# The opening of a transformer block on Trainium2: the modulation's last two column quarters multiplied in a row, the lower bounds in a buffer of their own, a sum in place of a maximum

## The chip, the cores and the metric

The kernel runs on one core of one Trainium2 chip. The metric is the device time of one execution in microseconds (us), the median of several executions. Five engines work side by side, each in the order of its own queue: TensorE (PE, matrix products and transposes, with its weight loads as PEld), VectorE (DVE), ScalarE (ACT), GpSimd (POOL) and SyncE (SP, which here only issues DMA transfers). They wait for each other through semaphores.

## The reference

One block of a diffusion transformer: 2048 tokens of width 1024, 256 tokens of context. A modulation vector is computed from a condition `c` (and from `c_ctx` for the context). It shifts and scales the normalized rows, which then go through a wide projection into two kinds of gated recurrences, an output projection, and a convolutional feed-forward part. What the change touches is the head of it:

```python
mod_x = (jax.nn.silu(c) @ w_mod[layer] + b_mod[layer])[:, None, :]
mod_c = jax.nn.silu(c_ctx) @ w_mod[layer] + b_mod[layer]
sh1, sc1, g1, sh2, sc2, g2 = jnp.split(mod_x, 6, axis=-1)
csh1, csc1, ... = jnp.split(mod_c, 6, axis=-1)
hx = _rmsnorm(x, norm1_g[layer]) * (1.0 + sc1) + sh1
feats_x = _mixer_features(hx, w_in[layer], lb, (rows, cols))   # p = h @ w_in, split into heads
```

`lb`, the lower bounds of the forget gates, is a softmax over two entries of `hgrn_lb`. The projection and the feed-forward products are done by the kernel with fewer block products (blocks of the operands are added and subtracted first), and each float32 operand is split into two float16 parts, so that a product is three float16 products.

## The kernel before

The rows are worked in four groups of 512 (`G`). The last group, rows 1536 to 2047 (called x3 here), is the first one used. Before the first projection can begin, the following is done.

- **Loads** (`setup`, `mod_loads`): SP issues, in this order, the first head's weights "z" (two tiles of `w_in`), the columns of `w_mod` that the first modulation needs in four quarters of 512 columns (`j4` = 2, 3, 0, 1; four tiles of 512 KB each), with x3 behind quarter 2 and the head's weights "q" and "vg" (three tiles, 1.5 MB) behind quarter 3. The context rows and the next group of rows come after.
- **Products** (`mod_first`, L284): eight per quarter, of the condition vectors against a weight tile, packed four at a time into 32-column strips of PE, in float32 (each shows as two instructions). The operand `silb` lies in a buffer with the tag "Tb".
- **Row copy and turn** (`mod_rows`, L249): ACT copies the quarter's result out of PSUM (L255, tile `modrow`), PE turns it into columns and adds the four strips (L260, `modt_ps`), DVE adds the bias and writes `modT` (L263). Quarters 0 and 1 give the shift, 2 and 3 the scale.
- **Lower bounds** (`lower_bounds`, L229): three DVE operations, an exponential on ACT, one small activation that brings the sigmoid's table back, and four DVE operations. Their buffer `tmp` has the tag "Tb" too, of which there is one.
- **Normalized rows** (`norm_rows`, L386): ACT squares x3 with sums (L398, eight), DVE adds them (L402), POOL takes the reciprocal root, DVE and ACT scale the rows (L409, L407).
- **Weights of the head** (`head_weights`, L720): per set, squares with sums on ACT (L749), a sum over the partitions on PE (`allsum`, L124), a power of two as scale (`pow2`, L112 to L116, on DVE), and then each block split into two float16 parts by ACT (L702, L759) and DVE (L703, L760), with sums and differences of blocks (L547 to L556) between.
- **Modulation** (`modulation`, L347): from `modT`, the factor U, a bound on the largest feature (`modq`, L361 to L369), its maximum over the partitions (`allmax`: a product with the identity, L138, a reduction, L140, and a product that spreads it, L142), and a power of two from it, `p2s`.
- **First features** (`first_blocks`, L419): eight groups of four transposes on PE (L416, three PSUM banks with the tag "pj"), each evicted with factor and shift by ACT (L459, six of them) or DVE (L457, two), in the order of blocks 0, 4, 1, 5, 2, 6, 3, 7; then the split of each block by ACT (L435, needs `p2s`) and DVE (L436), with block differences (L442). The first projection's products (L101 to L103) take these features.

The program is written in one order, and a planner then lays out each engine's queue from it: it plays the program against its own costs and gives an engine, at each moment, the earliest instruction of the program that is ready by that reckoning. On the chip each engine keeps the order so planned. `issue_after(i)` queues an instruction behind `i` on its engine, without a wait for its result. Tiles with the same tag share a fixed number of buffers, and a new tile waits until an older one has been read for the last time.

`heads` (L1038) calls these parts in the order: z weights; quarter 2 with its small vectors; lower bounds; x3's normalization; quarter 3; q and vg weights; quarter 0; quarter 1; modulation; first features.

Of the kernel before, what the change touches and what calls it, by code (L numbers as in the profile page):

```python
# [9 lines left out]
F32 = mybir.dt.float32  # L10
# [8 lines left out]
P = 128  # L19
# [4 lines left out]
NG = SEQ // G  # L24
# [26 lines left out]
def view(t, off, dims):  # L51
    return bass.AP(t.tensor, t.offset + off, [t.ap[0]] + dims)


class Kern:
# [173 lines left out]
    def lower_bounds(self):  # L229

        nc = self.nc
        a = view(self.sv, V_LB, [[8, 2], [1, 4]])
        b = view(self.sv, V_LB + 4, [[8, 2], [1, 4]])
        tmp = self.mp.tile([P, 24], F32, tag="Tb", bufs=1, name="tmp")
        m = tmp[:, 0:8].rearrange("p (d h) -> p d h", d=2)
        e = tmp[:, 8:24].rearrange("p (s d h) -> p s d h", s=2, d=2)
        nc.vector.tensor_tensor(m, a, b, ALU.max)
        nc.vector.tensor_tensor(e[:, 0], a, m, ALU.subtract)
        nc.vector.tensor_tensor(e[:, 1], b, m, ALU.subtract)
        nc.scalar.activation(e, e, AF.Exp)  # L240

        nc.scalar.activation(self.wp.tile([P, 1], F32, tag="rk", bufs=2, name="table"), e[:, 0, 0, 0:1], AF.Sigmoid)
        nc.vector.tensor_tensor(m, e[:, 0], e[:, 1], ALU.add)
        nc.vector.reciprocal(m, m)
        nc.vector.tensor_tensor(self.lb, e[:, 0], m, ALU.mult)
        nc.vector.tensor_scalar(self.omlb, self.lb, -1.0, 1.0, ALU.mult, ALU.add)


    def mod_rows(self, rows, nr, j4):  # L249


        nc = self.nc
        if nr == 2:
            rs = self.mp.tile([P, 512], F32, tag="Kl", bufs=KL, name="modrow")
            nc.scalar.copy(rs, rows)  # L255
            rows = rs
        ps = self.ps("tu", [P, 4, 2], "modt_ps")
        for j in range(4):
            sel = self.sel if nr == 2 else self.ones
            nc.tensor.matmul(ps[:, j, :nr], rows[:, j * P:(j + 1) * P], sel, start=True, stop=True, skip_group_check=True)  # L260
        o = self.modT[:, :nr, 4 * j4:4 * j4 + 4].rearrange("p d j -> p j d")
        bm = view(self.sv, V_BM + 4 * j4, [[1, 4], [0, nr]])
        nc.vector.tensor_tensor(o, ps[:, :, :nr], bm, ALU.add)  # L263

    def mod_loads(self):

        nc = self.nc
        self.items0[0][0]()
        self.wm = {}
        for j4, places in ((2, ("hx",) * 4), (3, ("hx",) * 4), (0, KEPT[:4]), (1, ("FG", "KTt", "ou0", "ou1"))):  # L270
            self.wm[j4] = []
            for k, tag in zip(range(0, KT, 2), places):
                w = self.slot_tile([P, 2, 512], F32, tag, "wm")
                nc.sync.dma_start(w, self.I["w_mod"][j4, :, k:k + 2])
                self.wm[j4] += [w[:, i] for i in range(2)]
            if j4 == 2:
                place = [h.rearrange("p k a t -> p (k a t)").bitcast(F32) for h in self.hc]
                place.append(self.slot_tile([P, G], F32, "qs", "x3"))
                self.x3 = self.load_rows(NG - 1, place)
            if j4 == 3:  # L280
                self.items0[4][0]()
                self.items0[5][0]()

    def mod_first(self, j4):  # L284

        nc = self.nc
        ps = self.ps("sc", [P, 512], "mod_ps")
        for k, w in enumerate(self.wm[j4]):
            q = k % 4 * B
            nc.tensor.matmul(ps[q:q + B], self.silb[:, k], w, start=k < 4, stop=k >= 4, skip_group_check=True)  # L290
        if j4 == 2:
            self.small_vectors()
        self.mod_rows(ps, 2, j4)

    def mod_later(self, j4):

# [50 lines left out]
    def modulation(self, cpool, pool, gain, sc, sh, dqcol, room=1.0):  # L347

        nc = self.nc
        n = gain.shape[-1]  # L350
        shp = list(sc.shape)
        A = cpool.tile(shp, F32, name=f"A{dqcol}")
        B = cpool.tile(shp, F32, name=f"B{dqcol}")
        U = pool.tile(shp, F32, tag="ra", bufs=4, name="modu")
        nc.vector.tensor_scalar(U, sc, 1.0, None, ALU.add)
        nc.vector.tensor_tensor(U, U, gain, ALU.mult)
        j = pool.tile(shp, F32, tag="ra", bufs=4, name="modj")
        q = pool.tile([P, 2], F32, tag="wdq", bufs=4, name="modq")
        ax = mybir.AxisListType.XY if len(shp) == 3 else mybir.AxisListType.X
        for i, (v, n) in enumerate(((U, 2.0 * D), (sh, 2.0))):  # L360
            nc.vector.scalar_tensor_tensor(j, v, n * room ** 2, v, ALU.mult, ALU.mult)  # L361
            nc.vector.tensor_reduce(q[:, i:i + 1], j, ax, ALU.add)
        if dqcol:

            sb = pool.tile([P, 1], F32, tag="edge", bufs=2, name="sumb")
            nc.vector.tensor_copy(sb, self.allsum(q[:, 1:2]))
            nc.vector.tensor_tensor(self.xx, self.allmax(q[:, 0:1]), sb, ALU.add)
            nc.vector.tensor_scalar(self.xx, self.xx, 1.03 / room ** 2, None, ALU.mult)
        nc.vector.tensor_tensor(q[:, 0:1], q[:, 0:1], q[:, 1:2], ALU.add)  # L369
        s, i = self.pow2(self.wp, self.allmax(q[:, 0:1]), 1, "w")  # L370
        nc.vector.tensor_copy(self.dqx[:, dqcol:dqcol + 1], i)
        self.plain = U, sh, s
        nc.vector.tensor_scalar(A, U, s, None, ALU.mult)
        nc.vector.tensor_scalar(B, sh, s, None, ALU.mult)
        return A, B, None
# [43 lines left out]
    def first_blocks(self, g, xn, places, bank, plain=False):  # L419
# [3 lines left out]
        nc = self.nc  # L423
# [20 lines left out]
        A, B, s = self.plain if plain else self.mod1  # L444
        late, b = [], []
        for k0 in (0, 2):
            f = [places[k0 + r]() for r in range(2)]
            units = [(slice(k0, k0 + 2), f)] if len(f[0]) == len(f[1]) == 1 else [(slice(k0 + i, k0 + i + 1), []) for i in range(2)]
            for i in range(2):
                k = k0 + i  # L450
                at = [(v[0][:, i] if len(v) == 1 else v[i])[:, :2 * n] for v in f]
                for r in range(2):
                    kk = k + 4 * r
                    tp = self.transposed(xn, kk, bank)
                    ka, kb = (v[:, which, kk:kk + 1] for v in (A, B))
                    if r and (g is None or plain and i):
                        nc.vector.tensor_scalar(at[r], tp, ka, kb, ALU.mult, ALU.add)  # L457
                    else:
                        nc.scalar.activation(at[r], tp, AF.Identity, bias=kb, scale=ka)  # L459
                if len(units) == 2 or i:  # L460
                    u = units[i if len(units) == 2 else 0][0]
                    both = [v[0][:, :, :2 * n] for v in f] if len(units) == 1 else [view(v, 0, [[0, 1], [1, 2 * n]]) for v in at]
                    b.append((u, [both[r][:, :, c * n:(c + 1) * n] for r in range(2) for c in range(2)]))
                    for r in range(2):
                        late.append((r, u, both[r][:, :, :n]))
                        if not plain:
                            pair(*late.pop())
                yield
# [569 lines left out]
    def heads(self):  # L1038

        nc, pool = self.nc, self.mp  # L1040
        W, items = self.W0, self.items0
        for _, comp in items[:4]:
            comp()
        self.mod_first(2)
        self.lower_bounds()
        self.norm_rows(NG - 1, self.x3)
        self.mod_first(3)
        for _, comp in items[4:]:
            comp()
        self.mod_first(0)  # L1050
        self.mod_first(1)
        place = [self.gate_tile() for _ in range(4)]
        xc = self.load_rows(None, place)
        self.mod1 = self.modulation(self.ep, pool, view(self.sv, V_N1, [[0, 2], [1, 8]]), self.modT[:, :, 8:16],
# [10 lines left out]
        rows = lambda g, tags: self.norm_rows(g, self.load_rows(g, [p() for p in self.places(tags, f"x{g}")]), self.tail)  # L1065
# [4 lines left out]
        for s in range(4 * 2 * NH):  # L1070
            h, i = divmod(s, NG)
# [922 lines left out]
```

## Time and profile before

| | |
|---|---|
| median of 3 executions | 2602.67 us (2600.81 to 2603.92) |
| profiled execution, its own time | 2600.32 us |
| its span, first to last instruction | 2598.5 us |
| mean granted TensorE clock | 0.985 |
| PE busy | 2509.5 us, 97% of the span |
| DVE busy | 1894.8 us, 73% |
| ACT busy | 1351.5 us, 52% |
| first product of the first projection | 55.04 us after the start |

How to read the lines: a timeline row gives the start and the duration in us, the engine, the line of the kernel, the operation, the tile written and the tiles read, the shapes, how many such instructions follow each other, and in brackets how long the engine had been idle and what ended that. A grouped row gives, after the bar, the busy time in us, the mean of one in ns, and the idle time ahead of it.

### The profile page before, as it was taken

The page shows a single profiled execution, that of the slowest core. Times are in us where ns is not written, and L with a number is a line of the kernel's source. Part 1 is how long each engine was busy: PE and PEld are TensorE (multiplying, and loading weights), DVE is VectorE, ACT ScalarE, POOL GpSimd, SP SyncE. Part 2 cuts the span into 40 slices and gives each one's busy share as a digit, 9 for nine tenths or more (in the row PEclk, how much of TensorE's full clock was granted, in tenths as well). Part 3 has the DMA queues.
Part 4 walks back from the last instruction along what each step waited for, and adds up shares of the span by engine and source line. Part 5 has one row for each costly group of instructions (what it writes and reads, how often), then busy time and mean ns, then how long its engine had stood idle before and what let it go on. Part 6 is the DMA issues. An engine that isn't in the chain of part 4 may idle for free.

```text
span 2598.5 us, 56251 instructions
## 1 busy us (share of the span) xinstructions
PE 2509.5 (97%) x22763; PEld 1655.1 (64%) x22763; DVE 1894.8 (73%) x4304; ACT 1351.5 (52%) x2880; POOL 383.0 (15%) x377
## 2 busy tenths in 40 slices
PE   6899998999999999999999999999999999999998
PEld 3688987889899999895544444444444444444443
DVE  5798686786878778885659787888888887223756
ACT  6886566564655454553647455556655554211221
POOL 1100000000000000001132343434443442000000
PEclk6999999999999999999999999999999999999999
DMA  7334342442558667794421333333333326544552
GB/s 304 118 114 153 119 144 87 136 155 67 180 163 280 213 220 251 247 331 148 169 82 43 128 104 108 101 111 114 102 106 110 122 90 246 196 173 154 211 212 84
DMA packets 144788, 402.36 MB, mean 155 GB/s; under 512 B 16143, under 2 KB 16371, under 8 KB 139920
## 3 DMA queue, kind: packets, MB, share of 16 engines
q1 hardware_dynamic: 134976, 381.81, 42.4%
q10 hardware_dynamic: 9248, 16.79, 2.0%
q8 instruction: 178, 2.92, 0.5%
q14 instruction: 82, 0.67, 0.1%
q0 software_dynamic: 304, 0.17, 0.0%
HBM read 302.77 MB, written 95.94 MB: 153 GB/s over the span
## 4 chain that ended last, share of the span: by engine, by line
PE 72%; DVE 11%; issue 6%; DMA 5%; ACT 4%; POOL 1%; SPq 0%; ACTq 0%; DVEq 0%; POOLq 0%
PE pa L101 8%; PE pa L102 8%; PE pa L103 8%; PE pd L103 5%; PE pd L101 5%; PE pd L102 5%; PE pc L101 4%; PE pc L103 3%; PE pc L102 3%; PE pb L101 2%; PE pb L102 2%; PE pb L103 2%; PE opp L101 2%; PE opp L103 2%; PE opp L102 2%
## 5 line engine op out<-in xcount | busy, mean ns | idle before, releaser
L101 PE MATMUL pa<-feat,w 128*128 128x512 f16 x704 | 265.0, 381 | 7.2 <-DVE tb L637 4.1
L103 PE MATMUL pa<-feat,w 128*128 128x512 f16 x704 | 267.9, 381 | 1.3 <-DVE w L703 1.3
L102 PE MATMUL pa<-feat,w 128*128 128x512 f16 x704 | 268.1, 381 | 0.0
L102 PE MATMUL pd<-wd,actl 128*128 128x512 f16 x616 | 233.3, 379 | 0.0
L103 PE MATMUL pd<-wd,actl 128*128 128x512 f16 x616 | 233.3, 379 | 0.0
L101 PE MATMUL pd<-wd,actl 128*128 128x512 f16 x616 | 232.7, 379 | 0.0
L103 PEld LDWEIGHTS <-w 128*128 128x128 f16 x1232 | 120.8, 98 | 149.9 <-DVE w L703 4.3
L102 PEld LDWEIGHTS <-w 128*128 128x128 f16 x1232 | 120.7, 98 | 149.1 <-issue 10.4
L101 PEld LDWEIGHTS <-w 128*128 128x128 f16 x1232 | 120.7, 98 | 141.6 <-issue 2.7
L102 PEld LDWEIGHTS <-hx 128*128 128x128 f16 x1824 | 179.5, 98 | 5.5 <-issue 3.5
L101 PEld LDWEIGHTS <-hx 128*128 128x128 f16 x1824 | 180.0, 99 | 2.2
L103 PEld LDWEIGHTS <-hx 128*128 128x128 f16 x1824 | 179.6, 99 | 0.9
L1470 POOL TENSOR_TENSOR ssq<-ssq 128x1 f32<-128x1 f32 x16 | 6.6, 415 | 1127.2 <-ACT junk L1465 1127.2
L1715 ACT ACTIVATE st<-act,modT 128x512 f16<-128x512 f32 x154 | 107.3, 717 | 112.4 <-DVE act L1705 60.8
L1716 DVE SCALAR_TENSOR_TENSOR st<-act,modT,st 128x512 f16<-128x512 f32 x154 | 143.9, 967 | 29.0 <-ACT st L1715 28.5
L101 PE MATMUL pa<-w_vg,hx 128*128 128x128 f16 x800 | 141.9, 219 | 0.5 <-ACT ct L603 0.2
L102 PE MATMUL pa<-w_vg,hx 128*128 128x128 f16 x800 | 141.8, 219 | 0.0
L103 PE MATMUL pa<-w_vg,hx 128*128 128x128 f16 x800 | 141.7, 219 | 0.0
L103 PE MATMUL pc<-feat,w 128*128 128x512 f16 x352 | 133.3, 379 | 2.0 <-DVE w L703 2.0
L101 PE MATMUL pc<-feat,w 128*128 128x512 f16 x352 | 133.4, 379 | 0.3 <-ACT tb L603 0.3
L102 PE MATMUL pc<-feat,w 128*128 128x512 f16 x352 | 133.4, 379 | 0.0
L101 PE MATMUL pa<-hx,w_z 128*128 128x256 f16 x464 | 127.3, 274 | 0.9 <-DVE K L645 0.6
(552 smaller groups left out, 7315.3 us busy)
## 6 DMA issues: line engine op xcount, KB each, us to landing
hx<-hxd SPq DMA_DIRECT2D x212, 512.0 KB, 5.1
actd<-st SPq DMA_DIRECT2D x154, 256.0 KB, 2.0
actl<-actd SPq DMA_DIRECT2D x28, 1024.0 KB, 5.2
wur<-in_w_up_dram SPq DMA_DIRECT2D x44, 512.0 KB, 3.5
raw<-in_w_in_dram SPq DMA_DIRECT2D x36, 512.0 KB, 4.5
wm<-in_w_mod_dram SPq DMA_DIRECT2D x64, 256.0 KB, 3.9
hxd<-hx SPq DMA_DIRECT2D x28, 512.0 KB, 4.8
wdb<-in_w_down_dram SPq DMA_DIRECT2D x44, 256.0 KB, 4.0
```

Of the source, the lines that this page charges most:

```text
L101: mm(ps, lhs(0), rhs(0), start=start, stop=False, skip_group_check=True)
L102: mm(ps, lhs(0), rhs(1), start=False, stop=False, skip_group_check=True)
L103: mm(ps, lhs(1), rhs(0), start=False, stop=stop, skip_group_check=True)
L1470: nc.gpsimd.tensor_tensor(ssq[:, 0:1], ssq[:, 0:1], ssq[:, 1:2], ALU.add)
L1715: nc.scalar.activation(p[:, 0], v, AF.Copy, scale=s)
L1716: nc.vector.scalar_tensor_tensor(p[:, 1], v, s, p[:, 0], ALU.mult, ALU.subtract)
```

## The change

Six things are altered.

1. `mod_first` only issues its products and gives back the PSUM tile. `heads` now calls the products of quarters 0 and 1 in a row, and after both their row copies and turns. Quarters 2 and 3 keep theirs directly behind.
2. The row copy of quarter 0 is done by DVE instead of ACT.
3. The lower bounds' buffer takes the tag "Ta" instead of "Tb".
4. The loads of the q and vg weights are issued behind quarter 2, ahead of x3 and quarter 3, instead of behind quarter 3; their computation is called ahead of x3's normalization and of quarter 3, instead of behind both.
5. The first modulation's scale is taken from the sum over the partitions (`allsum`) instead of the maximum (`allmax`); the second modulation keeps the maximum. The sum is a looser bound, so the scale can be a smaller power of two.
6. In the first features of x3, the groups of transposes from the fourth on are queued on PE behind the last turn's product.

```diff
@@ lower_bounds
-        tmp = self.mp.tile([P, 24], F32, tag="Tb", bufs=1, name="tmp")
+        tmp = self.mp.tile([P, 24], F32, tag="Ta", bufs=1, name="tmp")
@@ mod_rows
-            nc.scalar.copy(rs, rows)
+            if j4:
+                nc.scalar.copy(rs, rows)
+            else:
+                nc.vector.tensor_copy(rs, rows)
...
-            nc.tensor.matmul(ps[:, j, :nr], rows[:, j * P:(j + 1) * P], sel, start=True, stop=True, skip_group_check=True)
+            self.moded = nc.tensor.matmul(ps[:, j, :nr], rows[:, j * P:(j + 1) * P], sel, start=True, stop=True, skip_group_check=True)
@@ mod_loads
             if j4 == 2:
+                self.items0[4][0]()
+                self.items0[5][0]()
                 place = [h.rearrange("p k a t -> p (k a t)").bitcast(F32) for h in self.hc]
                 place.append(self.slot_tile([P, G], F32, "qs", "x3"))
                 self.x3 = self.load_rows(NG - 1, place)
-            if j4 == 3:
-                self.items0[4][0]()
-                self.items0[5][0]()
@@ mod_first
-        if j4 == 2:
-            self.small_vectors()
-        self.mod_rows(ps, 2, j4)
+        return ps
@@ modulation
-        s, i = self.pow2(self.wp, self.allmax(q[:, 0:1]), 1, "w")
+        s, i = self.pow2(self.wp, (self.allmax if dqcol else self.allsum)(q[:, 0:1]), 1, "w")
@@ first_blocks
-                    tp = self.transposed(xn, kk, bank)
+                    with self.tc.issue_after(self.moded.ins) if plain and k + r > 1 else nullcontext():
+                        tp = self.transposed(xn, kk, bank)
@@ heads
-        self.mod_first(2)
+        r2 = self.mod_first(2)
+        self.small_vectors()
+        self.mod_rows(r2, 2, 2)
         self.lower_bounds()
-        self.norm_rows(NG - 1, self.x3)
-        self.mod_first(3)
         for _, comp in items[4:]:
             comp()
-        self.mod_first(0)
-        self.mod_first(1)
+        self.norm_rows(NG - 1, self.x3)
+        self.mod_rows(self.mod_first(3), 2, 3)
+        rows = [self.mod_first(j) for j in range(2)]
+        for j in range(2):
+            self.mod_rows(rows[j], 2, j)
```

## The prediction, made before the change was run

> **What bounds the kernel now.** I began with the page, to see which engine carries the span:
>
> ```profile
> PE 2509.5 (97%) x22763; PEld 1655.1 (64%) x22763; DVE 1894.8 (73%) x4304; ACT 1351.5 (52%) x2880; POOL 383.0 (15%) x377
> ```
>
> TensorE (PE) is busy 97% of the span, so a change far off its path is worth nothing. The diff touches only the opening, before the first projection. There I read the timeline of PE alone; the columns are start, duration, instruction, count, and in brackets the idle time before it with what ended it:
>
> ```profile
> 25.72 0.33 PE L416 MATMUL tp<-ident,hc 128*128 128x128 f32 x1 [2.09 <-DVE hc L409]
> 25.98 1.05 PE L290 MATMUL mod_ps<-wm,silb 128*32 128x512 f32 x4
> ...
> 32.28 3.64 PE L290 MATMUL mod_ps<-wm,silb 128*32 128x512 f32 x16
> 36.62 1.87 PE L260 MATMUL modt_ps<-sel,modrow 128*128 128x2 f32 x8 [0.70 <-ACT modrow L255]
> 38.42 3.63 PE L290 MATMUL mod_ps<-wm,silb 128*32 128x512 f32 x12
> 41.97 0.90 PE L416 MATMUL tp<-ident,hc 128*128 128x128 f32 x3
> 42.67 0.42 PE L416 MATMUL tp<-ident,x 128*128 128x128 f32 x1
> 43.02 1.55 PE L290 MATMUL mod_ps<-wm,silb 128*32 128x512 f32 x4
> 44.50 0.66 PE L416 MATMUL tp<-ident,hc 128*128 128x128 f32 x4
> 45.26 1.05 PE L260 MATMUL modt_ps<-sel,modrow 128*128 128x2 f32 x8
> 47.46 0.90 PE L416 MATMUL tp<-ident,hc 128*128 128x128 f32 x3 [1.14 <-ACT ftmp L459]
> 48.15 0.42 PE L416 MATMUL tp<-ident,x 128*128 128x128 f32 x1
> 49.64 1.76 PE L416 MATMUL tp<-ident,hc 128*128 128x128 f32 x7 [1.07 <-ACT ftmp L459]
> 51.19 0.42 PE L416 MATMUL tp<-ident,x 128*128 128x128 f32 x1
> 51.54 0.59 PE L138 MATMUL row<-ident,modq 128*1 128x128 f32 x2
> 52.70 0.58 PE L142 MATMUL allmax<-allmax,ones 1*128 1x1 f32 x2 [0.57 <-DVE allmax L140]
> ```
>
> The products of column quarter 0 (16 from 32.28) are followed by that quarter's turn (L260, 36.62) and only then by the products of quarter 1 (12 from 38.42), whose last four start at 43.02 behind a group of four transposes and end at 44.57. VectorE (DVE) shows what hangs on them:
>
> ```profile
> 47.49 0.17 DVE L263 TENSOR_TENSOR modT<-modt_ps,sv 128x8 f32<-128x8 f32 x1
> ...
> 54.08 0.15 DVE L116 TENSOR_SCALAR p2s<-p2i 128x1 int32<-128x1 int32 x1
> ...
> 55.02 1.41 DVE L436 SCALAR_TENSOR_TENSOR hx<-ftmp,p2s,hx 128x512 f16<-128x512 f32 x2 [0.18 <-ACT hx L435]
> ```
>
> The modulation is complete at 47.66 (47.49 + 0.17), the scale p2s at 54.23, and only then can the splits of the features (L436) start. Grouped by line over 53 to 70 us:
>
> ```profile
> L436 DVE SCALAR_TENSOR_TENSOR hx<-ftmp,p2s,hx 128x512 f16<-128x512 f32 x14 | 9.8, 746 | 0.2 <-ACT hx L435 0.2
> L442 DVE TENSOR_TENSOR ftmp<-ftmp 128x512 f32<-128x512 f32 x8 | 5.2, 685 | 0.0
> ```
>
> Fourteen splits and eight block sums leave DVE 0.2 us idle: from 55.02 DVE is the bound, and PE waits for features. Nothing in that stretch hangs on a clock of its own, so an earlier start moves everything behind it. My yardstick is the second split of the pair, which starts at 55.68 (55.02 + 1.41 - 0.75).
>
> **What cannot move.** The last weight tile of quarter 1 is a DMA; the rows are those of the tile wm, over 0 to 60 us and over the last issue alone:
>
> ```profile
> L274 SPq DMA_DIRECT2D wm<-in_w_mod_dram x16: 327/328/498, 2.1 to 26.5; - x16
> ```
> ```profile
> DMA to landing us min/median/max: 11.6/11.6/11.6
> ```
> ```profile
> 27.01:44.07 17.07, 16.36 (x71) 9.09 (x69) 10.84 (x33) 12.36 (x21) 0.00 (x0) 0.50 1.04 399
> ```
>
> Issued at 26.5 it lands 11.6 later, at 38.1. The row of a stretch (busy time of PE, its loads, DVE, ACT, POOL; then PE clock 0.50, DMA share 1.04, 399 GB/s) shows the DMA engines full. The change moves the three tiles of w_in (1.5 MB, for q and vg) from behind quarter 3 to ahead of x3 and quarter 3, but all of it stood ahead of quarters 0 and 1 already: 38.1 stays. x3 and quarter 3 land later by 1.5 MB at 399 GB/s, 3.9 us.
>
> **The change, part by part.**
> *Products in a row.* Quarter 1's products no longer have quarter 0's turn ahead of them in the program, and the fourth and fifth groups of transposes (41.97 and 44.50) are queued behind the last turn. PE's own floor: 32.28 + 2 x 3.64 = 39.6, below the DMA's. The last four products are two of the four steps of such a 3.64, at this clock 1.8: 38.1 + 1.8 = 39.9 in place of 44.57, a gain of 4.6.
>
> *Row copies.* The copies' rows, with those of ScalarE's (ACT) other work between 13.9 and 56:
>
> ```profile
> L459 ACT ACTIVATE ftmp<-tp,modT,modu 128x512 f32<-128x512 f32 x6 | 4.4, 769 | 0.6 <-PE tp L416 0.5
> L398 ACT ACTIVATE junk<-hc 128x512 f16<-128x512 f32 x7 | 4.3, 621 | 0.1
> L702 ACT ACTIVATE w_vg<-raw,p2s 128x512 f16<-128x512 f32 x6 | 4.2, 717 | 1.7 <-DVE raw L547 1.1 <-DVE raw L556 0.5
> L702 ACT ACTIVATE w_z<-raw,p2s 128x512 f16<-128x512 f32 x4 | 2.9, 714 | 1.6 <-DVE raw L547 1.6
> L255 ACT COPY modrow<-mod_ps 128x512 f32<-128x512 f32 x4 | 2.3, 573 | 2.3 <-PE mod_ps L290 2.3
> ...
> L398 ACT ACTIVATION_READ_ACCUMULATOR junk<-hc 128x1 f32 x7 | 1.3, 186 | 0.0
> ```
>
> Quarter 1's stays on ACT, 0.57 and two hand-overs, 0.7: 40.6. Quarter 0's goes to DVE, where the trace has no such copy. From below its cost on the path is 0 (DVE is done with it while PE is on quarter 1), from above one split of 0.75 ahead of it and 0.75 of its own, which counts only if the turn of quarter 0 stands ahead of products in PE's order. I take 0, because 1.8 us of products cover it, and price the other as a rival.
>
> *Turns.* Eight at the half clock cost 1.87 (36.62): 42.5. At 45.26 they cost 1.05, since the clock was up. Then modT, 0.3 with its wait: 42.8, in place of 47.66.
>
> *Lower bounds.* They were held until the last product (44.57) by a buffer shared with the products' operand, and put two table loads between the copies and the evictions of the transposes:
>
> ```profile
> 25.18 1.95 ACT L407 ACTIVATE hc<-hc,rs_y 128x512 f32<-128x512 f32 x3 [2.77 <-POOL rs_y L76]
> ...
> 45.23 1.28 ACT L240 ACT_TABLE_LOAD   x1
> ...
> 47.42 1.28 ACT L242 ACT_TABLE_LOAD   x1
> ```
>
> These 2.56 us and two small activations (3.0 together) move ahead of x3's squares. That unblocks the modT addition, which stood on DVE behind the bounds (turns done at 46.31, modT begun at 47.49), and lets PE's waits of 1.14 and 1.07 for evictions shrink. What is late next is x3, below.
>
> *Sum for max.* From modT to the bound modq are three small DVE operations, 0.2 each as modT's own, with a hand-over 0.7: 43.5. Before, the row product L138 began only at 51.54, in PE's order behind eight transposes, and with the reduction and the second product it took until 53.28. The sum is one product like L142, 0.58. Of the five groups queued behind the last turn, two find a free PSUM bank (quarter 0's evictions need only quarter 0) and may go first, at 0.98 each (49.64 to 51.61 for two): 42.5 + 1.96 = 44.5, sum done 45.1. Scale: 53.28 to 54.23 is 0.95, so 46.05. That is 8.2 earlier.
>
> *What then binds.* Three groups of transposes remain: 45.1 + 2.9 = 48.0, the next to last at 47.1. ACT evicts that one in 0.77 (L459) to 47.9 and casts it in 0.72 (a float16 write like L702's) to 48.6. DVE evicts the last group itself, at ACT's price to 48.8, and then begins the second split. **Gain: 55.68 - 48.8 = 6.9.** An eviction of quarter 0 (0.77) may stand ahead of quarter 1's row copy; I take half of it off: **6.5 us.**
>
> *x3 behind the weights.* The squares of q and vg and their splits now come first in the program. ACT from 13.9: four splits of z 2.9, three squares of weights 3.7 (twice x3's elements, so 1.24 each, an estimate), a row copy 0.6, tables 3.0, nine splits of q and vg 6.4, then x3's eight squares 6.5 (0.62 and 0.19 each). If all of that goes first, the squares are complete at 37.0 instead of 22.41 (25.18 - 2.77); at best that stays, with x3's later load in the place of ACT's queue. From the last square to the scaling ACT sat idle 2.77 (before 25.18), so the scaling begins between 25 and 39.8. The first three groups of transposes then cost nothing, or begin half a us later (as 25.72 after 25.18), end at 40.3 + 3.0 = 43.3 and push the turns from 40.6 to 43.3, 2.7 later. So the forecast's own bounds are gains of 3.8 and 6.9.
>
> The profiled execution took 2600.32 around its span of 2598.5, which would give 2593.8. It lies 2.35 under the median of 2602.67, so for the median I say **2596.2**.
>
> **Rivals.**
> *The turn of quarter 0 stays in between* (0.20). The planned order had it there (36.62) and the program does not forbid it. Products of quarter 0 end at 35.9, copy 0.8, turn 1.87, products 3.64: 42.3, or 2.4 later than above: a gain of 4.1, 2598.6. For it: quarter 1 was taken by the planner to land late, since it let transposes in at 41.97. Against: the turn's data now come later in the program.
>
> *PE runs at full speed here* (0.13). With the rows at full clock (four products 1.05 at 25.98, turns 1.05 at 45.26, a group 0.66 at 44.50): 39.15, copy 39.85, turns 40.9, modT 41.2, modq 41.9, two groups 42.2, sum 42.8, two groups more 44.1, eviction 44.9, cast 45.6: a gain of 10.1, 2592.6. Against: clock 0.50 over 17 us with PE busy 16.36 of 17.07. [...]
>
> *Given back later* (0.10). The planner orders everything by its own times; a shifted opening can reorder the stages behind. I have no row for its size; taking half the gain, 2599.4. Against: DVE's 22 operations follow each other with 0.2 us idle.
>
> *Slower: x3's transposes ahead of the products* (0.07). If the planner puts the first three groups ahead of quarter 0's products, PE, which works in order, waits for x3. With the rows scaled from 39.8: transposes 40.3 to 43.3, two quarters of products 50.6, a turn 52.4, then the 8.9 from last product to second split (48.8 - 39.9): 61.3, 5.6 later than 55.68, **2608.3**. It decides from where the first scaled tile comes after 34.5, squares complete at 31.3. For it: at 25.72 PE did wait 2.09 for x3 with four products queued behind. Against: quarter 0's products, which found their weights without a wait at 32.28, would have to be planned after rows that come 7 us later.
>
> **How the numbers follow.** The forecast has 0.50. No change is what stays within 0.2%, 5.2 us, about what a measurement of this kernel can tell. Of the forecast's 0.50, 0.44 lies beyond it and 0.06 within, by its bounds of 3.8 to 6.9; with the full clock's 0.13 and 0.02 of the two middle cases, faster has 0.59. The rest of the two middle cases (0.28) and the 0.06 are within, with 0.01 of the last: 0.35. Slower keeps 0.06. The range takes in the full clock below and the two middle cases above, with the 1.5 us by which the runs shown scatter: 2592.0 to 2602.5.
>
> **What would show it.** Right: the last L290 product of the opening ends near 40 and not 44.6; no table load between 30 and 60; one product of L124 where L138 and L142 were; the scale near 46; DVE's first L436 near 48 and its 22 operations as dense as before. Wrong: L260 between the last two quarters' products; PE waiting for L409 or L407 past 35; the first L436 after 52. If the splits start near 48 and the time is yet the same, it was given back later.

## The result and the profile after

The changed kernel takes 2598.81 us (median of 20 executions, 2594.33 to 2602.55), the kernel before 2603.07 in 20 executions beside it (2598.86 to 2608.16). The ratio is 0.9982, 95% interval [0.9975, 0.9989]: some 4.7 us gained, between 2.9 and 6.5. The forecast was a gain of 6.5 us; the time lies in the range and nearer to its upper end, and the way there was not the one forecast. By the prediction's own line between faster and no change, 0.2% or 5.2 us, a gain of 4.7 is on the side of no change, which had 0.35.

The profiled execution of the changed kernel took 2600.73 us with a span of 2599.0, that of before 2600.32 with 2598.5. Two single executions say nothing on 4.7 us, since executions of one kernel lie 8 to 9 us apart. What the traces can say is where the opening gained and lost. First PE's timeline after the change (L292 are the products, L263 the turns, L416 the transposes, L124 the sum):

```profile
24.91 3.55 PE L292 MATMUL mod_ps<-wm,silb 128*32 128x512 f32 x12
33.72 0.92 PE L416 MATMUL tp<-ident,hc 128*128 128x128 f32 x3 [5.26 <-DVE hc L409]
34.57 1.92 PE L292 MATMUL mod_ps<-wm,silb 128*32 128x512 f32 x4
36.42 1.97 PE L416 MATMUL tp<-ident,hc 128*128 128x128 f32 x8
38.32 1.11 PE L292 MATMUL mod_ps<-wm,silb 128*32 128x512 f32 x4
...
39.53 0.95 PE L263 MATMUL modt_ps<-sel,modrow 128*128 128x2 f32 x8
40.41 1.92 PE L292 MATMUL mod_ps<-wm,silb 128*32 128x512 f32 x16
43.11 1.05 PE L263 MATMUL modt_ps<-sel,modrow 128*128 128x2 f32 x8 [0.78 <-DVE modrow L258]
44.10 1.91 PE L292 MATMUL mod_ps<-wm,silb 128*32 128x512 f32 x12
46.69 1.05 PE L263 MATMUL modt_ps<-sel,modrow 128*128 128x2 f32 x8 [0.69 <-ACT modrow L256]
...
48.71 0.35 PE L124 MATMUL allsum<-modq,ones 128*128 128x1 f32 x2
```

PE stands idle for 5.26 us until x3 is scaled, with the last four instructions of quarter 3's products and the first of quarter 0's queued behind. The last product ends at 46.01 (44.10 + 1.91), 1.4 later than before (44.57) and not 4.7 earlier. The turn of quarter 0 (43.11) stands between two stretches of quarter 1's products, with a wait of 0.78 for DVE's row copy. But from 38.5 on the rows run at full speed: 16 instructions take 1.92 where they took 3.64. Between 14 and 70 us PE stood at the half clock (0.50) for 23.9 us, before for 41.0; the mean there is 0.79, before 0.63. Over 2600 us, 17 us less at half clock raise the mean clock by 0.003. By as much the mean granted clock of the executions differs (0.989 in the changed kernel's 20, 0.986 in the 33 of before beside the first experiments), so the higher clock is not that of the profiled execution alone. The rows of two stretches, in the same columns as before, have the clock (1.00, and later 0.50):

```profile
38.48:55.50 17.02, 12.53 (x92) 7.40 (x91) 11.45 (x35) 10.46 (x16) 0.00 (x0) 1.00 0.57 214
...
62.40:65.80 3.40, 3.38 (x17) 2.40 (x17) 3.40 (x6) 3.34 (x8) 0.00 (x0) 0.50 0.32 130
```

On DVE the scale and the splits answer to the lines of before:

```profile
47.78 0.17 DVE L266 TENSOR_TENSOR modT<-modt_ps,sv 128x8 f32<-128x8 f32 x1 [3.41 <-PE modt_ps L263]
...
49.96 0.15 DVE L116 TENSOR_SCALAR p2s<-p2i 128x1 int32<-128x1 int32 x1
...
51.02 0.75 DVE L436 SCALAR_TENSOR_TENSOR hx<-ftmp,p2s,hx 128x512 f16<-128x512 f32 x1 [0.30 <-ACT hx L435]
...
52.41 0.74 DVE L436 SCALAR_TENSOR_TENSOR hx<-ftmp,p2s,hx 128x512 f16<-128x512 f32 x1
...
67.96 0.42 DVE L585 TENSOR_TENSOR ct<-ct,p 128x256 f32<-128x256 f32 x1 [2.04 <-PE p L103]
```

The second split, the yardstick, starts at 52.41 instead of 55.68: 3.3 earlier. From the last product to it pass 6.4 us; before it was 11.1 (55.68 - 44.57). So the opening lost 1.4 ahead of the last product and gained 4.7 behind it. In the last row DVE waits 2.04 us for PE, which ran at clock 0.50 again shortly before (62.40 to 65.80, busy for 3.38 of 3.40).

Why x3 is late is read on ACT, where the first square of x3 starts at 20.21 behind the three squares of q and vg (before: at 14.54) and two table loads stand between the squares, and in the scaling, which waits for POOL's reciprocal root:

```profile
20.21 0.61 ACT L398 ACTIVATE junk<-hc 128x512 f16<-128x512 f32 x1
...
21.40 1.28 ACT L240 ACT_TABLE_LOAD   x1
...
23.54 1.28 ACT L242 ACT_TABLE_LOAD   x1
...
28.70 0.63 ACT L398 ACTIVATE junk<-x 128x512 f16<-128x512 f32 x1
...
33.17 1.95 ACT L407 ACTIVATE hc<-hc,rs_y 128x512 f32<-128x512 f32 x3 [0.69 <-POOL rs_y L76]
```

The squares end at 29.42 (with the read of the sum behind the last), before at 22.41; the scaling begins at 33.17, before at 25.18. The forecast's bounds for both (22.41 to 37.0, and 25 to 39.8) held them.

### The profile page after: what moved, and what is told of

It reads as the page before. It is cut to its first block, busy times and chain, and to the rows that moved or that the text cites. A ratio compares the mean times of both kernels' runs of the same rounds, so it can differ in the third digit from the quotient of the medians.

```text
span 2599.0 us, 56245 instructions
## 1 busy us (share of the span) xinstructions
PE 2500.6 (96%) x22761; PEld 1647.9 (63%) x22761; DVE 1895.5 (73%) x4304; ACT 1351.0 (52%) x2879; POOL 385.4 (15%) x377
## 4 chain that ended last, share of the span: by engine, by line
PE 72%; DVE 11%; issue 6%; ACT 5%; DMA 5%; POOL 1%; SPq 0%; ACTq 0%; DVEq 0%; POOLq 0%
PE pa L101 8%; PE pa L102 8%; PE pa L103 8%; PE pd L102 5%; PE pd L101 5%; PE pd L103 5%; PE pc L101 3%; PE pc L103 3%; PE pc L102 3%; PE pb L101 2%; PE pb L102 2%; PE pb L103 2%; DMA raw<-in_w_in_dram 2%; PE opp L101 2%; PE opp L103 2%
## 5 line engine op out<-in xcount | busy, mean ns | idle before, releaser
L704 DVE SCALAR_TENSOR_TENSOR w<-wur,p2s,w 128x512 f16<-128x512 f32 x132 | 122.8, 938 | 6.0 <-ACT w L703 6.0
```

Source lines behind the costliest of these rows:

```text
L704: nc.vector.scalar_tensor_tensor(W[m][:, 1], v, sc, W[m][:, 0], ALU.mult, ALU.subtract)
```

## The experiments

Each kernel is compared with the kernel before on the same chip (the fifth to the eighth ran on another chip than the rest). The changed kernel's own ratio, 0.9982 [0.9975, 0.9989], is the measure for the undoings. "Opening" is by how much the operations between 40 and 80 us come earlier in the profiled execution than in that of before (median over the operations of DVE and ACT that both have): 3.3 us for the changed kernel. It is the shift of one execution against another.

### x3 and its normalization ahead of the q and vg weights again

```diff
@@ mod_loads, on the changed kernel
             if j4 == 2:
-                self.items0[4][0]()
-                self.items0[5][0]()
...
+            if j4 == 3:
+                self.items0[4][0]()
+                self.items0[5][0]()
@@ heads
-        for _, comp in items[4:]:
-            comp()
         self.norm_rows(NG - 1, self.x3)
         self.mod_rows(self.mod_first(3), 2, 3)
+        for _, comp in items[4:]:
+            comp()
```

> All of the change but its fourth part: the q and vg weights are loaded and worked behind quarter 3 again, as before. Theory A (x3 behind the weights ate part of the gain): in the changed kernel the scaling of x3 began at 33.17 instead of 25.18 and TensorE idled 5.26 us for it; with the weights' three squares (3.7 us) behind x3 again the scaling begins near 28 to 29, the last modulation product ends near 41 to 42 instead of 46.0, the splits start near 48, and the kernel is 2 to 3 us faster than the changed one, so 6 to 7 us faster than before. Theory B (late x3 cost nothing, because the work piled up behind it ran densely and raised the clock to full from 38.5 on): with x3 early the turns and transposes run at the half clock again, the splits start near 51, and the kernel is within 1 us of the changed one, 4 us faster than before.

Measured: 2600.81 us, 0.9990 [0.9982, 0.9999]; opening 0.3 us earlier than before. PE's timeline:

```profile
28.68 0.48 PE L417 MATMUL tp<-ident,hc 128*128 128x128 f32 x1 [4.84 <-DVE hc L410]
...
36.26 3.64 PE L293 MATMUL mod_ps<-wm,silb 128*32 128x512 f32 x16
41.55 1.87 PE L263 MATMUL modt_ps<-sel,modrow 128*128 128x2 f32 x8 [1.65 <-DVE modrow L258]
43.34 3.64 PE L293 MATMUL mod_ps<-wm,silb 128*32 128x512 f32 x16
47.69 1.87 PE L263 MATMUL modt_ps<-sel,modrow 128*128 128x2 f32 x8 [0.71 <-ACT modrow L256]
```

```profile
27.80:55.10 27.30, 23.71 (x103) 15.30 (x104) 17.15 (x56) 18.37 (x29) 0.22 (x2) 0.50 0.75 288
```

x3 came 5.0 us earlier (28.68 for 33.72), and nothing was gained by it: the splits of q and vg now stand among the row copies on DVE (a wait of 1.65), and PE ran 27.3 us at the half clock though busy for 23.71 of them. The last product ends at 46.98, later than with the late x3. So "x3 late" is not by itself what limits the gain; here the half clock and the order of the copies stood in its place (with the turns moved as well, under "x3 first and the turns behind", the products end at 40.86). By the traces part 4 of the change is worth 3.0 us of the opening within the whole (0.3 for 3.3); the intervals of the two ratios overlap.

### Both turns behind the last product

```diff
@@ mod_first, on the changed kernel
-            nc.tensor.matmul(ps[q:q + B], self.silb[:, k], w, ...)
+            self.prod = nc.tensor.matmul(ps[q:q + B], self.silb[:, k], w, ...)
@@ heads
-            self.mod_rows(rows[j], 2, j)
+            with self.tc.issue_after(self.prod.ins):
+                self.mod_rows(rows[j], 2, j)
```

> The changed kernel, with both turns queued on TensorE behind the last product of quarter 1. In the changed kernel quarter 0's turn stood behind the first two products of quarter 1, with 0.78 us of waiting for the row copy on DVE and 1.05 us of its own. Theory A (the turn in between lies on the path): the last product ends 1.8 us earlier, the last turn follows with both turns in a row, 0.9 us longer, so the splits start 0.9 us earlier and the time falls by about 1 us. Rival (the end is set elsewhere, by TensorE's clock and by DVE behind it): the splits move but the time stays within 0.5 us.

Measured: 2596.76 us, 0.9978 [0.9969, 0.9987]; opening 5.4 us. PE, with L263 now one run of 16:

```profile
39.67 3.63 PE L292 MATMUL mod_ps<-wm,silb 128*32 128x512 f32 x28
43.23 1.95 PE L263 MATMUL modt_ps<-sel,modrow 128*128 128x2 f32 x16
```

```profile
50.28 0.74 DVE L436 SCALAR_TENSOR_TENSOR hx<-ftmp,p2s,hx 128x512 f16<-128x512 f32 x1
...
64.20 0.42 DVE L585 TENSOR_TENSOR ct<-ct,p 128x256 f32<-128x256 f32 x1 [0.42 <-PE p L103]
```

28 product instructions without a gap end at 43.30 instead of 46.01, and the second split starts 2.1 us earlier than in the changed kernel, where 0.9 was expected. This is the products in a row that the change names and the planner did not give. The time's interval overlaps that of the changed kernel, so the 2 us are shown in the trace and only indicated in the time; it lies under both kernels' medians.

### The two small parts alone

```diff
@@ modulation, on the kernel before
-        s, i = self.pow2(self.wp, self.allmax(q[:, 0:1]), 1, "w")
+        s, i = self.pow2(self.wp, (self.allmax if dqcol else self.allsum)(q[:, 0:1]), 1, "w")
```

> The kernel before, with the sum over the partitions instead of the maximum in the first scale and nothing else. The planned order leaves the sum behind all transposes, where the row product stood (51.54). Theory A: the reduction and the second product go (51.54 to 53.28 becomes 0.6), but DVE's last eviction ends only at 52.46, so the scale comes 0.8 us earlier and the time falls by 0.8 us, not more. Rival (each part is worth what it takes off its own chain): 1.2 us or more.

Measured: 2598.91 us, 0.9993 [0.9982, 1.0003]; opening 0.7 us.

```diff
@@ lower_bounds, on the kernel before
-        tmp = self.mp.tile([P, 24], F32, tag="Tb", bufs=1, name="tmp")
+        tmp = self.mp.tile([P, 24], F32, tag="Ta", bufs=1, name="tmp")
```

> The kernel before, with the lower bounds in their own buffer and nothing else. The planned order then has the eight products of quarter 1 without transposes between. Theory A (the two table loads stood between the last product and the features): tables and bounds run ahead of 30 us, x3 is scaled up to 3 us later, the last product ends 1 us earlier, the evictions follow without 2.56 us of table loads, the splits start 2 to 3 us earlier and the time falls by 2 to 3 us. Rival (the three microseconds of ACT only move in front of x3 and come back as late transposes): 0 to 1 us.

Measured: 2600.95 us, 0.9996 [0.9987, 1.0005]; opening 1.3 us. The scale's row of each, the sum first:

```profile
53.36 0.15 DVE L116 TENSOR_SCALAR p2s<-p2i 128x1 int32<-128x1 int32 x1
```

```profile
52.72 0.15 DVE L116 TENSOR_SCALAR p2s<-p2i 128x1 int32<-128x1 int32 x1
```

Against 54.08 before, the sum is worth 0.7 and the bounds' buffer 1.4. Neither shows in the time alone.

### x3 first and the turns behind

This joins the first two edits.

> As the run with x3 first (the change without its fourth part), and both turns queued behind the last product of quarter 1. With x3 first TensorE waited 1.65 us for the row copy on DVE ahead of quarter 0's turn, and stayed at the half clock from 27.8 to 55.1. [...]

Measured: 2602.38 us, 0.9998 [0.9990, 1.0006]; opening 2.85 us.

```profile
35.54 5.32 PE L293 MATMUL mod_ps<-wm,silb 128*32 128x512 f32 x32
40.79 1.05 PE L263 MATMUL modt_ps<-sel,modrow 128*128 128x2 f32 x8
45.19 1.34 PE L263 MATMUL modt_ps<-sel,modrow 128*128 128x2 f32 x8 [3.35 <-ACT modrow L256]
```

The 32 product instructions end at 40.86, close to the 39.9 of the forecast. Then quarter 1's turn waits 3.35 us for its row copy: ACT is behind the splits of vg, and it copies from 44.57. The early end of the products is spent in ACT's queue. That the ratio shows none of the 2.85 us of the opening is not explained by this.

### Quarter 0's products ahead of x3's transposes

```diff
@@ first_blocks, on the kernel with the turns behind
-                    with self.tc.issue_after(self.moded.ins) if plain and k + r > 1 else nullcontext():
+                    with self.tc.issue_after((self.moded if k + r > 1 else self.prod0).ins) if plain else nullcontext():
@@ heads
-        rows = [self.mod_first(j) for j in range(2)]
+        rows = [self.mod_first(0)]
+        self.prod0 = self.prod
+        rows.append(self.mod_first(1))
```

> As the run with both turns behind, and the first three groups of x3's transposes queued behind quarter 0's products. In the changed kernel four products of quarter 3 and all of quarter 0 stood on TensorE behind x3, 5.26 us idle. Theory A (that order, not the load, made the products late): quarters 3 and 0 are done by 33, the transposes end near 37, quarter 1 ends near 40 where its load lets it, the splits start near 46 to 47, and the time is 2 us below the run with the turns behind, 7 to 8 below before. Theory B (the dense run behind the late x3 is what raises the clock; spread out, the same work stays at the half clock): the last product ends near 41, but turns and transposes take twice as long, the splits start near 49 and the time is that of the run with the turns behind.

Measured: 2600.76 us, 0.9983 [0.9974, 0.9992]; opening 3.5 us.

```profile
35.82 1.87 PE L263 MATMUL modt_ps<-sel,modrow 128*128 128x2 f32 x8 [6.31 <-ACT modrow L256]
...
43.37 1.92 PE L292 MATMUL mod_ps<-wm,silb 128*32 128x512 f32 x16
```

PE did not wait for x3 any more, but for 6.31 us for the row copy of quarter 3, which ACT makes behind x3's squares and scaling. The products end at 45.29. One wait took the other's place, and neither of the two theories had it.

### The weights first, alone

The loads and the calls of q and vg are moved as in part 4, and nothing else.

> The kernel before, with the fourth part alone: the q and vg weights are loaded and worked ahead of x3. Theory A (late x3 is a loss of its own): x3 is scaled near 30 instead of 25.2, without the tables' 3 us, the last product ends 2 to 4 us later and the time rises by 1 to 3 us. Theory B (the work piled up behind x3 then runs at full clock): the last product ends later, but transposes and turns behind it take half, and the time stays within 1 us of before or falls.

Measured: 2602.12 us, 0.9993 [0.9984, 1.0002]. The opening came 2.4 us later than before (the scale at 56.47), and the time is not longer. In this execution the offset is +2.4 us between 100 and 120 us and -1.0 between 200 and 300; what takes it back there is left open.

### PE kept at work while x3 is scaled

```diff
@@ heads, on the kernel with x3 first
+        self.norm_rows(NG - 1, self.x3)
+        r3 = self.mod_first(3)
+        with self.tc.issue_after(self.fifth.ins):
+            idle = self.ps("tu", [P, P], "idle")
+            for _ in range(36):
+                self.warm = nc.tensor.transpose(idle, self.ident, self.ident)
+        self.mod_rows(r3, 2, 3)
...
-        self.norm_rows(NG - 1, self.x3)
-        self.mod_rows(self.mod_first(3), 2, 3)
```

The result of the 36 added transposes is not read; x3's own are queued behind them.

> As the run with x3 first, with 36 transposes of the identity matrix, whose result nobody reads, filling TensorE's idle 4.84 us ahead of x3's first transpose. Theory A (the clock is what held the run with x3 first back): TensorE is busy through the stretch from 24.4 to 27.8, the clock stays up behind it, products, turns and transposes take half of what they took, the last product ends near 42 instead of 47.0, and the time is 4 us below the run with x3 first. Theory B (row copies and loads set the end, not the clock): less than 1 us below it.

Measured: 2602.88 us, 0.9997 [0.9988, 1.0006]; opening 2.65 us later than before. PE's timeline, and a row of the stretch with the added transposes (columns as before):

```profile
33.91 1.05 PE L263 MATMUL modt_ps<-sel,modrow 128*128 128x2 f32 x8 [3.10 <-ACT modrow L256]
...
48.62 1.05 PE L263 MATMUL modt_ps<-sel,modrow 128*128 128x2 f32 x8 [2.06 <-ACT modrow L256]
```

```profile
24.60:34.90 10.30, 7.07 (x53) 5.44 (x52) 1.99 (x6) 7.50 (x15) 2.03 (x6) 1.00 1.03 412
```

The clock was 1.00 from 24.6 to 34.9, where with x3 first alone it was 0.50 from 27.8 to 55.1. But the planner laid ACT's queue out anew as well, and two turns wait 3.10 and 2.06 for row copies on ACT. The run does not price the clock by itself; it shows that in this kernel these 10.3 us at 1.00 bought nothing, with ACT's copies in the way.

### The table loads behind x3's squares

```diff
@@ lower_bounds, on the kernel with the turns behind
-        nc.scalar.activation(e, e, AF.Exp)
+        with self.tc.issue_after(self.sqlast.ins):
+            nc.scalar.activation(e, e, AF.Exp)
@@ heads
-        self.lower_bounds()
         for _, comp in items[4:]:
             comp()
         self.norm_rows(NG - 1, self.x3)
+        self.lower_bounds()
```

(`sqlast` is the last of x3's squares.)

> The kernel with the turns behind the last product, and besides the lower bounds' two table loads on ACT queued behind x3's last square instead of between the squares. Theory A (x3 still sets the opening, and the tables are part of what makes it late): the squares end near 26.6 instead of 29.4, DVE scales from about 30.3 instead of 33.1, the first transposes stand near 30.8, the last product of quarter 1 ends 1 to 2.5 us earlier than 43.3, the first split near 47; time 1 to 2 us under the 2596.8 of that kernel. Rival B (quarter 3's products were not the end any more, ACT's splits of q and vg or PE's clock take the place of x3): the transposes start earlier, the first split stays within 0.7 us of 48.9 and the time within 1 us.

Measured: 2596.18 us, 0.9976 [0.9967, 0.9986]; opening 5.2 us. DVE's timeline of this kernel, with the splits of vg (L705) and x3's scaling (L410):

```profile
31.20 0.75 DVE L705 SCALAR_TENSOR_TENSOR w_vg<-raw,p2s,w_vg 128x512 f16<-128x512 f32 x1 [1.25 <-ACT w_vg L704]
31.87 0.88 DVE L410 TENSOR_SCALAR hc<-hc,rs_y 128x512 f32<-128x512 f32 x2
```

The squares end at 26.29, 3.1 earlier, and the reciprocal root is ready at 30.0. But DVE had a split of vg queued ahead, which waited 1.25 for ACT, and ACT now did the tables there. Scaling begins 1.3 earlier and the last product ends at 43.55, no earlier than the 43.30 of the kernel with the turns behind. Behind the squares the tables are still ahead of x3's scaling, by way of that split, and the time is the same. The last run below takes them out of x3's way altogether.

### The maximum kept, and the bounds' buffer kept

Each undoes one part of the changed kernel: the maximum instead of the sum, and the tag "Tb" instead of "Ta".

> The changed kernel with the maximum over the partitions instead of the sum (three steps on PE and DVE instead of one). Theory A (the sum is worth what it saves on the chain from modT to the scale, about as when it was made alone): the scale 0.8 to 2 us later than 49.96, the splits by as much, time 1 to 2 us above the changed kernel's. Rival B (the second split waits for the last eviction and cast anyway, so the sum is covered): the scale comes later, but the second split stays within 0.4 us of 52.4 and the time is the changed kernel's.

Measured: 2599.19 us, 0.9987 [0.9978, 0.9996]; opening 2.05 us.

```profile
50.06 0.38 PE L142 MATMUL allmax<-allmax,ones 1*128 1x1 f32 x2
```

```profile
51.96 0.15 DVE L116 TENSOR_SCALAR p2s<-p2i 128x1 int32<-128x1 int32 x1
52.97 1.41 DVE L436 SCALAR_TENSOR_TENSOR hx<-ftmp,p2s,hx 128x512 f16<-128x512 f32 x2 [0.24 <-ACT hx L435]
```

The second product of the maximum starts 1.35 later than the sum did (48.71), the scale comes 2.0 later, and the second split, at 53.64 (52.97 + 1.41 - 0.74), 1.2 later. In the changed kernel the sum is thus worth 1.2 us in the opening; the ratios' intervals overlap and don't tell.

> The changed kernel with the lower bounds' buffer shared with the products' operand again, so that the table loads come after the last product. Theory A (the tables cost as much ahead of x3's squares as they cost in the tail): x3's first transposes about 2.5 us earlier than 33.7, the last product up to 2.5 us earlier than 46.0, the tail from there to the second split 2 to 3 us longer than 6.4: time within 1 us of the changed kernel's. Rival B (the tail is where they cost, and an earlier x3 buys nothing since PE falls to half clock or waits for the weights): the last product stays near 45 to 46, the second split comes 2 us or more after 52.4, time 2 to 3 us above the changed kernel's.

Measured: 2598.25 us, 0.9985 [0.9975, 0.9994]; opening 5.8 us.

```profile
40.12 1.91 PE L292 MATMUL mod_ps<-wm,silb 128*32 128x512 f32 x12
```

```profile
42.68 1.28 ACT L240 ACT_TABLE_LOAD   x1
...
44.21 1.28 ACT L242 ACT_TABLE_LOAD   x1
```

```profile
49.93 0.74 DVE L436 SCALAR_TENSOR_TENSOR hx<-ftmp,p2s,hx 128x512 f16<-128x512 f32 x1
```

With the tables back in the tail, x3's first transposes start at 30.41 instead of 33.72, the last product ends at 42.03, 4.0 us earlier, and the tail to the second split takes 7.9 instead of 6.4. The second split starts 2.5 us earlier than in the changed kernel. So the bounds' own buffer, worth 1.4 alone, costs the opening 2.5 once the weights stand ahead of x3: a part of the change that helps by itself hurts within the whole. The times cannot be told apart, and this edit together with the turns behind was not run.

## Why the prediction was right, and where it was not

**The sum.** Gain forecast 6.5 (6.9 by the yardstick), measured 4.7 in the time with 2.9 to 6.5, and 3.3 by the yardstick in one pair of profiles. The direction held, and the time fell into the range, but on another way. By the yardstick's own path the last product came 6.1 us later than in the sum and the tail was 2.5 shorter, so two errors offset each other in part; that the time lies 1.4 above the yardstick's 3.3 no trace explains. The range was met by luck as much as by the mechanism. What happened is three of the rivals together: the turn in between (0.20), the full clock (0.13) and x3's transposes ahead of products (0.07). Each was priced as if it came alone. The 0.06 of the forecast that was to lie within 5.2 us was also small for bounds that begin at 3.8.

**Products in a row: failed.** The last product was to end at 39.9 and ended at 46.0. Two steps of it failed. "PE's own floor 32.28 + 2 x 3.64" took quarter 0's products as where they had been; they began at 38.3, behind x3's transposes, because PE works in order and waited for x3 until 33.72. That is the place of the slower rival, in small: there x3's rows at 39.8 cost 5.6 us, here the scaling began at 33.17 and PE had its first tile at 33.72, ahead of the 34.5 from which it was to decide, and it cost the start of the products. And the turn of quarter 0 stayed in between, which was the first rival; undoing it showed what it cost: 2.7 us at the last product and 2.1 at the second split, close to the 2.4 worked out for it.

**The weights of the modulation: right.** The last tile's DMA was to land at 38.1 as before. The last of these issues started at 26.7, and none took more than 10.6 us to land, so it was there by 37.3; none of PE's waits from 38 on is for it.

**x3 behind the weights: bounds right, consequence wrong.** The scaling began at 33.17, 8.0 later than before. I let only the transposes and the turns suffer for it, and kept the products where they had been.

**Row copy of quarter 0 on DVE, costed at 0.** It cost a wait of 0.78 in front of the turn, since the turn stood ahead of products: the case that was priced as a rival. With x3 first it cost 1.65.

**Turns, sum and tail at the half clock: wrong in the gain's favour.** The tail was worked out as 8.9 us and took 6.4. The turns took 1.05 and not 1.87, a group of transposes about 0.5 instead of 0.98, since the clock was 1.00 from 38.48 to 55.50. The other part came as forecast: no L240 or L242 after 24.9, one L124 in place of two products, no wait of the modT addition for the bounds. The signs that were to stand at given times (last product near 40, scale near 46, first split near 48) all stand 3 to 6 us later, and the turn between the products, named as a sign of being wrong, is there.

**The full clock was given 0.13 on a wrong reading.** I set the row with PE busy 16.36 of 17.07 us at clock 0.50 against it, as if a busy PE at 0.50 would stay there. The rows of after don't bear that out: PE busy for 12.53 of 17.02 at 1.00, and for 3.38 of 3.40 at 0.50. Its 2592.6 did not come: the tail, at 1.00, took 6.4 us and not the 8.9 worked out for 0.50, and x3's wait took the products' start.

**Nothing in the stretch behind hangs on a clock of its own: wrong.** The clock is such a thing. 22 operations of DVE stayed as dense as forecast, and then its additions waited 2.04 (67.96) for a PE that had run at 0.50 from 62.40 to 65.80, where the kernel with the turns behind waited 0.42 (64.20): 3.8 us apart there, from 2.1 at the second split. How much of this belongs to one execution and how much to the kernel, two profiles cannot say.

Grouped by line from 48 to 66 us after the change:

```profile
L436 DVE SCALAR_TENSOR_TENSOR hx<-ftmp,p2s,hx 128x512 f16<-128x512 f32 x14 | 9.8, 745 | 0.3 <-ACT hx L435 0.3
L442 DVE TENSOR_TENSOR ftmp<-ftmp 128x512 f32<-128x512 f32 x8 | 5.1, 685 | 0.0
```

**What stays open.** The medians of before beside the experiments were 2601.80 (first four kernels), 2604.05 (the next four) and 2601.94 (the last three). Openings and gains of the medians agree within some 2 us for most kernels (3.3 and 4.3 for the changed one, 5.4 and 5.0 with the turns behind, 5.2 and 5.8 with the tables moved) and not for two: the weights first alone (2.4 later, 1.9 faster) and the busy PE (2.65 later, 1.2 faster). Behind the opening the offsets between two executions wander: the changed kernel's 3.3 us are 0.9 between 500 and 1000 us and gone at the end (spans of 2599.0 and 2598.5), and the 2.85 of x3 first with the turns behind become 6.0 the other way. The mean granted clock does not sort them (0.989 in the changed kernel's profile, 0.986 in that one, 0.987 with the turns behind, the shortest of the thirteen profiled executions). No run here settles what does, so the way from the opening to the time rests on the medians, and these tell few of the kernels apart.

## What to carry to other kernels

A stretch of program moved ahead is paid by what is queued behind it on in-order engines: follow each engine's next waiting instruction (here PE's x3 transposes ahead of the products, with a wait of 5.26 us) before taking an old start time over into a sum. Where a turn or a copy belongs to one of two runs of products, check in the planned order that it stands behind both, and say so to the planner if it does not. And before pricing a PE stretch at the clock it had, ask whether the change alters what runs in it: with x3 first, moving the turn out from between the products ended them 6.1 us earlier (40.86 for 46.98), with no work removed, and the 32 instructions took 5.32 us in place of twice 3.64. Last, undo the parts of a change one by one within the whole: the bounds' buffer was worth 1.4 us of the opening alone and cost 2.5 there.

## What the runs showed of the hardware

**PE's granted clock did not follow its busy time.** Stretches of the traces:

| kernel | stretch, us | PE busy, us | granted clock |
|---|---|---|---|
| before | 27.01 to 44.07 | 16.36 of 17.07 | 0.50 |
| before | 47.49 to 64.55 | 11.86 of 17.07 | 0.50 |
| changed | 38.48 to 55.50 | 12.53 of 17.02 | 1.00 |
| changed | 62.40 to 65.80 | 3.38 of 3.40 | 0.50 |
| x3 first | 27.80 to 55.10 | 23.71 of 27.30 | 0.50 |
| turns behind | 16.40 to 36.90 | 10.07 of 20.50 | 0.50 |
| turns behind | 36.90 to 47.10 | 10.01 of 10.20 | 1.00 |
| PE kept at work | 24.60 to 34.90 | 7.07 of 10.30 | 1.00 |
| tables moved | 38.60 to 48.90 | 9.68 of 10.30 | 1.00 |

PE was busy for 0.96 of a stretch at 0.50 (before, from 27.01) and for 0.69 of one at 1.00 (PE kept at work), and for 0.49 of one at 0.50 and 0.98 of one at 1.00 (both with the turns behind). What the clock costs is in the rows: 16 product instructions took 3.64 us at 0.50 (before, 32.28) and 1.92 at 1.00 (changed, 40.41), eight turns 1.87 (before, 36.62) and 1.05 (changed, 43.11). What raised it, and what let it fall back, no run shows.

**Three of POOL's small operations took longer beside DVE's splits.** The reciprocal root before, with DVE waiting for it (L74 and L75 took 0.20 each as well), and after, beside splits that read two tiles:

```profile
22.98 1.05 POOL L72 TENSOR_TENSOR rs_y<-rs_v,mhalf 128x4 f32<-128x4 f32 x1
24.10 0.20 POOL L73 TENSOR_TENSOR rs_t<-rs_y 128x4 f32<-128x4 f32 x1
```

```profile
29.99 1.05 POOL L72 TENSOR_TENSOR rs_y<-rs_v,mhalf 128x4 f32<-128x4 f32 x1
31.11 0.42 POOL L73 TENSOR_TENSOR rs_t<-rs_y 128x4 f32<-128x4 f32 x1
31.61 0.59 POOL L74 TENSOR_TENSOR rs_t<-rs_t,rs_v 128x4 f32<-128x4 f32 x1
32.28 0.57 POOL L75 TENSOR_SCALAR rs_t<-rs_t 128x4 f32<-128x4 f32 x1
```

Three operations of 0.20 took 1.58 us in place of 0.60. Of the 1.0 us more, x3's path holds at most what the scaling then waited for POOL: 0.37 on DVE, whose own splits end at 32.80, and 0.69 on ACT. L72, which reads two tiles as well, took its 1.05 beside the splits as without them. In the kernel with the tables moved the two that met DVE's splits took 0.72 and 0.66, and the two ahead of the splits 0.20 each. That the splits caused it was not shown.
